# Norms of the keys taken per pair of heads, group norm's Newton steps on GpSimd, and a token shift that reads the neighbouring chunk's bank

## The chip, the cores and the metric

The kernel runs on one core of a Trainium2 chip. A core has TensorE (PE, matrix products; PEld is its weight load, which overlaps), VectorE (DVE), ScalarE (ACT) and GpSimd (POOL). SyncE (SP) only issues transfers here, in the order of its queue. The metric is the device time of one execution in microseconds; the time before is a median of three, 1370.82 us (1363.31 to 1373.83).

## The reference

One layer of a hybrid decoder for a prompt of 1024 tokens and 8 sequences of 4 sample tokens: RWKV-7 time mixing beside dilated sliding-window attention, a gated merge and a closing layer norm, all in fp32. What the change touches:

```python
h = x @ w_in                                            # 1024 -> 9344 columns
prev = concat([shift_prev[:, None], zs[:, :-1]], axis=1)
zs_mixed = zs + mu_shift * (prev - zs)                  # token shift of r, k, v, decay, a
# rwkv_mix, 8 heads of 64 columns
kk = (k * k_k).reshape(B, T, 8, 64)
kk = kk / maximum(norm(kk, axis=-1, keepdims=True), 1e-12)   # keys' norm
k = k * (1.0 + (a - 1.0) * k_a)
S = (S * w_t + (S @ -kk_t) (kk_t * a_t) + v_t k_t)      # one state per head, token by token
o_t = S @ r_t
mu, var = mean(o), mean(square(o - mu))                 # over the 64 columns of a head
o = (o - mu) * rsqrt(var + GN_EPS) * lnx_g + lnx_b      # group norm
y = (o + bonus) * silu(z_gate)
```

## The kernel before

Columns lie on the 128 partitions and tokens along the free side; a tile of 128 columns holds two heads, a pair j of four. The 1056 tokens of prompt and samples are cut into three chunks of 352. The layer has three parts one after the other: the recurrent part (to about 620 us), attention (to about 1184) and the output. The change touches only the first.

A **product** is a group of matmuls at L173 of a 128-column block of the weights with the tokens. Numbers are split into a high and a low part, so three products make one exact one. Weights come by SP (L160) into two buffers `wraw`, are split by ScalarE (`whi`, L163) and VectorE (`wlo`, L164), and 24 matmuls per chunk add up in one of four PSUM banks `pj`. When a chunk is complete, its `consume` takes it out of the bank: `shifted` (L237 to L248) mixes each token with the one before, where the last column of a chunk is kept in a tile `lst` for the next (L239, L241); `silu` (L200) and `gate` (L306) send theirs to DRAM.

Beside the products run four streams, for 8 **units** (pair j, half hf of 512 tokens):

- `units`: `unit` makes the keys' norm (squares, small matmuls against `bones` at L321, `rsqrt` by a seed L151 and three Newton steps L153 to L155 on VectorE, a copy L328 that spreads each norm over its 64 columns, and four PE transposes L344 that turn this into the layout of the keys), the decay and `a` (the lora matmuls L301), then the operands BK (L346 to L355) and KR (L365, L366) and the products AT (L380 on PE, masked by L387 on VectorE; two banks `g` hold them, in two groups of 16 matmuls).
- `inverses`: a triangular inverse in 31 steps on VectorE (L452, L455), which goes through DRAM (Yd, Xd) into AT.
- `scans`: a transposed copy T of the inverse's part (L474), products with it on PE (L487 to L523), and then the scan: 8 chunks of 64 tokens, each with two **hops**. PE multiplies the state `st` with KR (L538), VectorE adds (W, L539), PE multiplies W with BT (L544), VectorE makes the new state in two operations (L547). PE and VectorE wait for each other here, and products are put between.
- `norms`: the group norm of a unit's output on VectorE (L569 to L580), with four PE transposes (L584) behind it.

The order of PE's work is fixed at build time by a planner. Each stream yields a pair: the time that it put on PE, and the time until its next piece is due; products fill what is left. The second number is where the constants stand (`D_KR`, `D_GN` and the like):

```python
streams, prods = [[0.0, scans()], [0.0, norms()], [0.0, inverses()], [0.0, units()]], products()
...
if x[0] <= now and (small < SMALL or x in own or not prods):
    r = next(x[1], 0)
    ...
    now += r[0]
    x[0] = now + r[1]
```

The other engines' order comes from a scheduler that follows what it takes to be ready; each engine, and SP's queue, runs its own strictly in that order. A tile of a pool with few buffers (`t` has six, `nt`, `so` and `srow` one) is waited for until its last reader is done.

Of the kernel before, what the change touches and what calls it, by code (L numbers as in the profile page):

```python
# [14 lines left out]
AF = mybir.ActivationFunctionType  # L15
ALU = mybir.AluOpType
AX = mybir.AxisListType

P = 128
D = 1024  # L20
KT = D // P
SEQ = 1024
# [10 lines left out]
D_PM, D_HOP, D_ST, D_GN, D_IN, D_U0, D_MASK = 0.9, 1.25, 1.75, 12.6, 11.0, 1.2, 1.2  # L33
# [51 lines left out]
def tile_layer(ctx: ExitStack, tc: tile.TileContext, A: dict, O: list):  # L85
# [64 lines left out]
    def rsqrt(y, x, t):  # L150
        V.tensor_scalar(y.bitcast(I32), x.bitcast(I32), -0.5, float(0x5F3759DF), ALU.mult, ALU.add)  # L151
        for _ in range(3):
            V.scalar_tensor_tensor(t, y, -0.5, x, ALU.mult, ALU.mult)  # L153
            V.tensor_tensor(t, t, y, ALU.mult)
            V.scalar_tensor_tensor(y, t, 1.5, y, ALU.add, ALU.mult)  # L155
# [74 lines left out]
    def shifted(s, M):  # L230
        mu, om = prm[:, MU + s : MU + s + 1], der[:, OMM + s : OMM + s + 1]
        lst = mk(rp, [P, 2], "lst", 2)

        def consume(c, b):
            n, t0 = npr(c), c * CH
            S.activation(M[:, t0 : t0 + n], b[:, 0:n], AF.Copy, scale=om)
            V.scalar_tensor_tensor(M[:, t0 + 1 : t0 + n], b[:, 0 : n - 1], mu, M[:, t0 + 1 : t0 + n], ALU.mult, ALU.add)  # L237
            if c:
                V.scalar_tensor_tensor(M[:, t0 : t0 + 1], lst[:, c - 1 : c], mu, M[:, t0 : t0 + 1], ALU.mult, ALU.add)  # L239
            if c < 2:  # L240
                V.tensor_copy(lst[:, c : c + 1], b[:, n - 1 : n])  # L241
            else:
# [69 lines left out]
    def unit(j, hf, M, st, out):  # L312
# [4 lines left out]
        sq = t_()  # L317
        S.activation(sq[:], Mk[:, sl], AF.Square, scale=prm[:, KK + j : KK + j + 1])
        pn = ps("g")
        for c2 in range(4):  # L320
            T.matmul(pn[:, 2 * c2 : 2 * c2 + 2], sq[:, c2 * P : (c2 + 1) * P], bones[:, 0:P:64], start=True, stop=True)  # L321
        yield (0.4, 0.6)
        nt = mk(rp, [P, 24], "nt", 1)
        n2, rn, tn = nt[:, 0:8], nt[:, 8:16], nt[:, 16:24]
        V.tensor_scalar(n2, pn[:, 0:8], 1e-24, None, ALU.max)
        rsqrt(rn, n2, tn)
        rb = t_()
        V.tensor_copy(rb.rearrange("p (a b) -> p a b", a=8), rn.unsqueeze(2).to_broadcast([P, 8, 64]))  # L328
        pw, pa = ps("g"), ps("g")
        lora(((pw[:], 0, j), (pa[:], 1, j)), sl)  # L330
        yield (1.3, D_PN)
        sg = t_()
# [8 lines left out]
        yield (0.0, D_KR)  # L341
        pn = ps("g")
        for c2 in range(4):
            T.transpose(pn[:, c2 * P : (c2 + 1) * P], rb[:, c2 * P : (c2 + 1) * P], ident)  # L344
        kkn = t_()
        V.scalar_tensor_tensor(kkn[:], Mk[:, sl], prm[:, KK + j : KK + j + 1], pn[:], ALU.mult, ALU.mult)  # L346
# [9 lines left out]
        yield (0.45, 0.0)  # L356
# [207 lines left out]
    def norm(j, hf, Ot, bon):  # L564
# [5 lines left out]
        V.tensor_scalar(m8[:], m8[:], 1.0 / 64.0, None, ALU.mult)  # L570
# [901 lines left out]
```

## Time and profile before

| | before |
|---|---|
| three runs | 1363.31, 1370.82, 1373.83 us |
| profiled execution | 1366.1 us |
| its span, first to last instruction | 1364.2 us |
| mean granted clock of PE | 0.994 |
| PE, VectorE, ScalarE, GpSimd busy | 97%, 59%, 34%, 5% |

The span is 1.9 us shorter than the profiled execution, and that execution lies 4.7 us below the median of the three. Rows of a timeline give start, duration, engine, line, operation, tiles written and read, shapes and a count; what stands in brackets is the idle time before it and what ended that. A wait is put down to what came last. Busy times of PE overlap slightly from row to row.

### The profile page before, as it was taken

Reading aid. Unit: us, or ns where it says so; the run is one execution under the profiler, and the core shown is the slowest. Engines: PE = TensorE matmul, PEld = TensorE weight load, DVE = VectorE, ACT = ScalarE, POOL = GpSimd, SP = SyncE. Lnnn points to the kernel's source line nnn. Section 1 sums busy time; section 2 is a strip of 40 time slices with the busy share of each in tenths; the row PEclk is TensorE's granted clock in tenths of the full one; section 3 lists DMA queues with packets and bytes.
Section 4 is the critical chain, followed back from the end, with each engine's and each line's share of the span. In section 5 each row is a group of like instructions: output and inputs, shape, how many; then the busy total and the mean of one; then the engine's idle time right before and its main releaser. Section 6 shows DMA issues by size and latency. Waiting matters only on the chain.

```text
span 1364.2 us, 25930 instructions
## 1 busy us (share of the span) xinstructions
PE 1328.3 (97%) x10097; PEld 1240.9 (91%) x10097; DVE 805.4 (59%) x2203; ACT 469.4 (34%) x1065; POOL 65.5 (5%) x82
## 2 busy tenths in 40 slices
PE   8999999999999999999999999999999999999997
PEld 7998999898988999999999999999999998899786
DVE  5677668786576855543554385437543844665565
ACT  5334344434443443422332323232332234132211
POOL 0000000000000000000000000000000000024100
PEclk9999999999999999999999999999999999999999
DMA  6122223122322233328545465545555656795221
GB/s 208 46 61 66 67 86 97 52 74 69 97 61 80 73 109 95 93 93 156 105 109 120 118 133 102 123 128 129 100 120 129 129 124 156 235 287 165 83 100 68
DMA packets 340151, 151.64 MB, mean 111 GB/s; under 512 B 188808, under 2 KB 329502, under 8 KB 339774
## 3 DMA queue, kind: packets, MB, share of 16 engines
q1 hardware_dynamic: 241150, 129.68, 34.9%
q10 hardware_dynamic: 98880, 20.32, 7.5%
q8 instruction: 79, 1.29, 0.4%
q14 instruction: 42, 0.34, 0.1%
HBM read 110.68 MB, written 38.97 MB: 110 GB/s over the span
## 4 chain that ended last, share of the span: by engine, by line
PE 80%; DVE 12%; DMA 4%; issue 1%; SPq 1%; ACT 1%; ACTq 0%; DVEq 0%
PE pj L173 58%; PE pj L1426 7%; PE o L980 2%; PE s L943 2%; DVE tm L452 2%; DVE X L455 2%; PE t L963 1%; PE g L380 1%; PE s L1062 1%; DMA wraw<-in_w_in_dram 1%; DVE wlo L164 1%; DVE st L547 1%; PE sc L538 1%; DMA cb<-cd 1%; PE sc L544 1%
## 5 line engine op out<-in xcount | busy, mean ns | idle before, releaser
L173 PE MATMUL pj<-xhi,whi 128*128 128x352 f32 x1848 | 398.2, 336 | 4.3 <-ACT xhi L1293 3.2
L173 PE MATMUL pj<-xhi,wlo 128*128 128x352 f32 x1848 | 386.2, 330 | 0.0
L173 PE MATMUL pj<-xlo,whi 128*128 128x352 f32 x1848 | 380.3, 327 | 0.0
L173 PEld LDWEIGHTS pj<-xhi,whi 128*128 128x128 f32 x1848 | 304.0, 189 | 20.5 <-issue 10.4
L173 PEld LDWEIGHTS pj<-xhi,wlo 128*128 128x128 f32 x1848 | 307.2, 190 | 3.9 <-issue 2.3
L173 PEld LDWEIGHTS pj<-xlo,whi 128*128 128x128 f32 x1848 | 308.8, 189 | 1.8 <-issue 0.7
L164 DVE TENSOR_TENSOR wlo<-wraw,whi 128x512 fp32r<-128x512 f32 x162 | 112.7, 697 | 89.8 <-ACT whi L163 89.2
L163 ACT ACTIVATE whi<-wraw 128x512 fp32r<-128x512 f32 x162 | 100.5, 625 | 132.8 <-PE pj L173 87.2
L953 ACT ACTIVATE Sm<-Sm,nm 128x128 f32<-128x128 f32 (+1 forms) x96 | 42.4, 442 | 101.9 <-DVE nm L950 101.9
L452 DVE TENSOR_TENSOR tm<-Y,X 128x60 f32<-128x60 f32 (+24 forms) x248 | 52.2, 210 | 11.1 <-DMA Y<-Yd 4.7
L455 DVE TENSOR_TENSOR X<-X,tm 128x60 f32<-128x60 f32 (+24 forms) x248 | 52.0, 210 | 6.0
L547 DVE SCALAR_TENSOR_TENSOR st<-sc,E,SD 64x64 f32<-64x64 f32 x128 | 36.1, 282 | 29.5 <-PE sc L544 27.8
L945 DVE CUSTOM_DVE_ANT_0 Sm<-s,cst 128x128 f32<-128x128 f32 (+1 forms) x96 | 29.2, 347 | 40.5 <-PE s L943 39.9
L1426 PE MATMUL pj<-wl,mh 128*128 128x512 f32 (+1 forms) x136 | 52.0, 382 | 0.0
L536 ACT ACTIVATE SD<-st,E 128x128 f32<-128x128 f32 x64 | 25.6, 400 | 71.0 <-DVE st L547 70.8
L806 POOL TENSOR_TENSOR kvp<-vv,kv 128x512 f32<-128x512 f32 x16 | 19.7, 1234 | 471.1 <-DVE Ss L814 387.8
L980 PE MATMUL o<-PT,Vt 128*128 128x128 f32 x280 | 38.8, 276 | 0.8 <-ACT PT L967 0.8
L868 ACT ACTIVATE k<-pj 128x352 f32<-128x352 f32 (+1 forms) x36 | 16.2, 454 | 66.1 <-PE pj L173 66.1
L943 PE MATMUL s<-k,q 128*128 128x128 f32 (+1 forms) x192 | 37.7, 325 | 0.7 <-DVE ml L945 0.7
L980 PEld LDWEIGHTS o<-PT,Vt 128*128 128x128 f32 x280 | 36.4, 191 | 1.5 <-ACT PT L967 1.1
L306 ACT ACTIVATE zt<-pj,der 128x352 f32<-128x352 f32 x48 | 26.5, 552 | 31.8 <-PE pj L173 26.5
L540 ACT ACTIVATE Ot<-sc 64x128 f32<-64x128 f32 x64 | 17.3, 270 | 53.3 <-DVE W L539 53.0
(320 smaller groups left out, 1697.6 us busy)
## 6 DMA issues: line engine op xcount, KB each, us to landing
wraw<-in_w_in_dram SPq DMA_DIRECT2D x146, 256.0 KB
gd<-zt SPq DMA_DIRECT2D x48, 176.0 KB
gt<-gd SPq DMA_DIRECT2D x48, 176.0 KB
vs<-bt ACTq DMA_DIRECT2D x48, 128.0 KB
kc<-in_cache_kv_g_dram SPq DMA_DIRECT2D x48, 128.0 KB
Vt<-vs ACTq DMA_DIRECT2D x12, 512.0 KB
cb<-cd SPq DMA_DIRECT2D x12, 512.0 KB
zd<-zt SPq DMA_DIRECT2D x24, 176.0 KB
```

The lines of the kernel that those rows point to most:

```text
L163: S.activation(hi[:], raw[:], AF.Copy)
L164: V.tensor_tensor(lo[:], raw[:], hi.bitcast(F32)[:], ALU.subtract)
L173: T.matmul(out, w[wi][:, n % 4, :], x[:, n % 4, :], start=first and n == 0, stop=last and n == 11)
L306: S.activation(t[:], b[:], AF.Tanh, scale=0.5, bias=der[:, HB + col : HB + col + 1])
L452: V.tensor_tensor(tm, Y[:, r : r + 1, r + 1 : 32].to_broadcast([P, m, n]), X[:, 0:m, r : r + 1].to_broadcast([P, m, n]), ALU.mult)
L455: V.tensor_tensor(X[:, 0:m, r + 1 : 32], X[:, 0:m, r + 1 : 32], tm, ALU.subtract)
L547: V.scalar_tensor_tensor(S1[d, d], pS[d, d], E[d, c, 64:65], SD[d, d], ALU.mult, ALU.add)
L943: T.matmul(r, qT[:, i * P : (i + 1) * P], kT[:, keys[i][0] * P : keys[i][0] * P + n], start=True, stop=True)
L945: V.tensor_tensor_reduce(out=Sm[:, i, 0:n], in0=r, in1=m3 if g == 2 else m12[:, 256 - n : 256], scale=1.0, scalar=NEG, op0=ALU.add, op1=AL ...
L953: S.activation(Sm[:, i, 0:n], Sm[:, i, 0:n], AF.Exp, scale=SCALE, bias=nm[:, x : x + 1], accum_out=ml[:, g, 1, i : i + 1])
L980: T.matmul(po[:, (i % 4) * P : (i % 4 + 1) * P], st["Vt"][:, kb_, :], PT[:, n * P : (n + 1) * P], start=m == 0, stop=m == len(keys[i]) - 1,)
L1426: T.matmul(pb[:], a[:, k], wk, start=x == 0, stop=x == len(prods) - 1)
```

## The change

Three things are changed.

*Keys' norm.* The squares' sums of both halves of a pair are taken together when the first half is due, 16 rows of 128 tokens in all; the tile is transposed by one matmul to [16 x 128], its reciprocal root is taken in that layout, and the result is written to DRAM (`nd`). Each half then reads it back by two transfers that broadcast one head's row over 64 partitions (`rb`). The copy and the four transposes are gone. The planner gets a new constant D_ROW for the time that the way takes.

*Group norm.* The division by 64 and the subtraction are one operation. The three Newton steps, four operations each, are on GpSimd; the seed and the multiply stay on VectorE, and the stream yields between them.

*Token shift.* The first column of a chunk reads the last column of the neighbouring chunk straight from that chunk's PSUM bank; the copies into `lst` are gone.

```diff
--- before.py
+++ after.py
@@ -30,7 +30,7 @@
 
 PIECE = 3
 D_PN, D_KR, D_AT, D_G, D_W, D_INV, D_UP = 0.65, 1.81, 4.5, 0.2, 2.09, 1.3, 8.4
-D_PM, D_HOP, D_ST, D_GN, D_IN, D_U0, D_MASK = 0.9, 1.25, 1.75, 12.6, 11.0, 1.2, 1.2
+D_PM, D_HOP, D_ST, D_GN, D_IN, D_U0, D_MASK, D_ROW = 0.9, 1.25, 1.75, 12.6, 11.0, 1.2, 1.2, 5.0
 SMALL = 1.0
 RS = 8
 CDEC = math.exp(-0.5)
@@ -147,9 +147,15 @@
             V.tensor_tensor(xlo[h][:, :, sl], bv, hi.bitcast(F32), ALU.subtract)
 
 
-    def rsqrt(y, x, t):
+    def rsqrt(y, x, t, pool=False):
         V.tensor_scalar(y.bitcast(I32), x.bitcast(I32), -0.5, float(0x5F3759DF), ALU.mult, ALU.add)
         for _ in range(3):
+            if pool:
+                G.tensor_tensor(t, y, y, ALU.mult)
+                G.tensor_tensor(t, t, x, ALU.mult)
+                G.tensor_scalar(t, t, -0.5, 1.5, ALU.mult, ALU.add)
+                G.tensor_tensor(y, y, t, ALU.mult)
+                continue
             V.scalar_tensor_tensor(t, y, -0.5, x, ALU.mult, ALU.mult)
             V.tensor_tensor(t, t, y, ALU.mult)
             V.scalar_tensor_tensor(y, t, 1.5, y, ALU.add, ALU.mult)
@@ -229,17 +235,16 @@
 
     def shifted(s, M):
         mu, om = prm[:, MU + s : MU + s + 1], der[:, OMM + s : OMM + s + 1]
-        lst = mk(rp, [P, 2], "lst", 2)
+        banks = {}
 
         def consume(c, b):
             n, t0 = npr(c), c * CH
+            banks[c] = b
             S.activation(M[:, t0 : t0 + n], b[:, 0:n], AF.Copy, scale=om)
             V.scalar_tensor_tensor(M[:, t0 + 1 : t0 + n], b[:, 0 : n - 1], mu, M[:, t0 + 1 : t0 + n], ALU.mult, ALU.add)
             if c:
-                V.scalar_tensor_tensor(M[:, t0 : t0 + 1], lst[:, c - 1 : c], mu, M[:, t0 : t0 + 1], ALU.mult, ALU.add)
-            if c < 2:
-                V.tensor_copy(lst[:, c : c + 1], b[:, n - 1 : n])
-            else:
+                V.scalar_tensor_tensor(M[:, t0 : t0 + 1], banks[c - 1][:, CH - 1 : CH], mu, M[:, t0 : t0 + 1], ALU.mult, ALU.add)
+            if c == 2:
                 bs = b[:, n:CH].rearrange("p (b t) -> p b t", t=NT)
                 ms = sM[:, s, :].rearrange("p (b t) -> p b t", t=NT)
                 S.activation(sM[:, s, :], b[:, n:CH], AF.Copy, scale=om)
@@ -314,21 +319,31 @@
         sl = slice(512 * hf, 512 * hf + 512)
         t_ = lambda tag="t", n=6: mk(rp, [P, 512], tag, n)
         c2p = lambda a: a.rearrange("p (a b c) -> p a b c", a=4, b=2)
-        sq = t_()
-        S.activation(sq[:], Mk[:, sl], AF.Square, scale=prm[:, KK + j : KK + j + 1])
-        pn = ps("g")
-        for c2 in range(4):
-            T.matmul(pn[:, 2 * c2 : 2 * c2 + 2], sq[:, c2 * P : (c2 + 1) * P], bones[:, 0:P:64], start=True, stop=True)
-        yield (0.4, 0.6)
-        nt = mk(rp, [P, 24], "nt", 1)
-        n2, rn, tn = nt[:, 0:8], nt[:, 8:16], nt[:, 16:24]
-        V.tensor_scalar(n2, pn[:, 0:8], 1e-24, None, ALU.max)
-        rsqrt(rn, n2, tn)
-        rb = t_()
-        V.tensor_copy(rb.rearrange("p (a b) -> p a b", a=8), rn.unsqueeze(2).to_broadcast([P, 8, 64]))
+
+        if hf == 0:
+            pn = ps("g")
+            for x in range(2):
+                sq = t_()
+                S.activation(sq[:], Mk[:, 512 * x : 512 * x + 512], AF.Square, scale=prm[:, KK + j : KK + j + 1])
+                for c2 in range(4):
+                    n = 4 * x + c2
+                    T.matmul(pn[:, n:16:8], sq[:, c2 * P : (c2 + 1) * P], bones[:, 0:P:64], start=True, stop=True)
+                yield (0.8, 0.4)
+            n2 = mk(rp, [P, 16], "n2", 1)
+            V.tensor_scalar(n2[:], pn[:, 0:16], 1e-24, None, ALU.max)
+            yield (0.0, 0.6)
+            pn = ps("g")
+            T.transpose(pn[0:16, 0:P], n2[:], ident)
+            yield (0.1, 0.4)
+            rn, tn = mk(rp, [P, P], "so", 1), mk(rp, [P, P], "srow", 1)
+            rsqrt(rn[0:16, :], pn[0:16, 0:P], tn[0:16, :])
+            SP.dma_start(nd[j].rearrange("e (c p) -> (e c) p", p=P), rn[0:16, :])
         pw, pa = ps("g"), ps("g")
         lora(((pw[:], 0, j), (pa[:], 1, j)), sl)
         yield (1.3, D_PN)
+        rb = t_()
+        for e in range(2):
+            SP.dma_start(rb[64 * e : 64 * e + 64, :], nd[j, e : e + 1, sl].to_broadcast([64, 512]))
         sg = t_()
         S.activation(sg[:], pw[:], AF.Tanh, scale=0.5, bias=der[:, HW0 + j : HW0 + j + 1])
         ta = t_()
@@ -338,12 +353,9 @@
         V.tensor_tensor_scan(lam[:], rmask, sg[:], 0.0, ALU.mult, ALU.add)
         Ei = t_()
         S.activation(Ei[:], lam[:], AF.Exp, scale=0.5 * CDEC)
-        yield (0.0, D_KR)
-        pn = ps("g")
-        for c2 in range(4):
-            T.transpose(pn[:, c2 * P : (c2 + 1) * P], rb[:, c2 * P : (c2 + 1) * P], ident)
+        yield (0.0, D_KR + D_ROW / 3 if hf else D_KR + D_ROW)
         kkn = t_()
-        V.scalar_tensor_tensor(kkn[:], Mk[:, sl], prm[:, KK + j : KK + j + 1], pn[:], ALU.mult, ALU.mult)
+        V.scalar_tensor_tensor(kkn[:], Mk[:, sl], prm[:, KK + j : KK + j + 1], rb[:], ALU.mult, ALU.mult)
         bt = t_()
         V.scalar_tensor_tensor(bt[:], ta[:], 1.0, kkn[:], ALU.add, ALU.mult)
         f2 = t_()
@@ -353,7 +365,6 @@
         BK = mk(rp, [P, 4, 4, 64], "BK", 1)
         V.scalar_tensor_tensor(BK[:, :, 1:3, :], c2p(bt), 0.5, c2p(Ei), ALU.mult, ALU.mult)
         V.tensor_tensor(BK[:, :, 0:4:3, :], c2p(k2), c2p(Ei), ALU.mult)
-        yield (0.45, 0.0)
         while done["scan"] < 2 * j + hf - 1 or 0 not in M:
             yield None
         Mr = M[0]
@@ -567,8 +578,7 @@
         Og = Ot.rearrange("p a (b c) -> p (a b) c", b=2)
         m8 = mk(rp, [P, 8], "m8", 1)
         V.tensor_reduce(m8[:], Og, AX.X, ALU.add)
-        V.tensor_scalar(m8[:], m8[:], 1.0 / 64.0, None, ALU.mult)
-        V.tensor_tensor(Og, Og, m8.unsqueeze(2).to_broadcast([P, 8, 64]), ALU.subtract)
+        V.scalar_tensor_tensor(Og, m8.unsqueeze(2).to_broadcast([P, 8, 64]), -1.0 / 64.0, Og, ALU.mult, ALU.add)
         sq = t_("sz", 2)
         S.activation(sq[:], Ot.rearrange("p a b -> p (a b)"), AF.Square)
         v8 = mk(rp, [P, 8], "v8", 1)
@@ -576,9 +586,10 @@
         V.tensor_scalar(v8[:], v8[:], 1.0 / 64.0, GN_EPS, ALU.mult, ALU.add)
         nt = mk(rp, [P, 24], "nt", 1)
         r8 = nt[:, 0:8]
-        rsqrt(r8, v8[:], nt[:, 8:16])
+        rsqrt(r8, v8[:], nt[:, 8:16], True)
+        yield (0.0, 3.0)
         V.tensor_tensor(Og, Og, r8.unsqueeze(2).to_broadcast([P, 8, 64]), ALU.mult)
-        yield (0.0, D_GN)
+        yield (0.0, D_GN - 3.0)
         po = ps("g")
         for c2 in range(4):
             T.transpose(po[:, c2 * P : (c2 + 1) * P], Ot[:, c2, :], ident)
@@ -606,6 +617,7 @@
     pbc = lambda o: prm[:, o : o + 4].unsqueeze(2).to_broadcast([P, 4, NS])
     dbc = lambda o: der[:, o : o + 4].unsqueeze(2).to_broadcast([P, 4, NS])
     bns = mk(cpool, [P, 4, NS], "bns")
+    nd = mk(dpool, [4, 2, SEQ], "nd")
     vd = mk(dpool, [8, NS, 6, 64], "vd")
```

The order on the engines, before and then after, at three places. First VectorE at the first unit's group norm. `Ot` is the unit's output, `v` the variance, `nt` the tile of the root, `AT` the masked products of a later unit, `zt` a gate and `wlo` a weight split. Before, with the last of the three Newton steps at its head:

```order
L153 SCALAR_TENSOR_TENSOR nt_2080<-nt_2080,v_371_2077 128x8
L154 TENSOR_TENSOR nt_2080<-nt_2080 128x8
L155 SCALAR_TENSOR_TENSOR nt_2080<-nt_2080 128x8
L580 TENSOR_TENSOR Ot_1568<-Ot_1568,nt_2080 128x512
L200 SCALAR_TENSOR_TENSOR zt_2134<-zt_2135,pj_2017 128x352
L387 TENSOR_TENSOR AT_2143<-g_2144,cst_76 128x512
L387 TENSOR_TENSOR AT_2143<-g_2145,cst_76 128x512
L200 SCALAR_TENSOR_TENSOR zt_2164<-zt_2165,pj_2018 128x352
```

and after:

```order
L586 TENSOR_SCALAR v_366_2056<-v_366_2056 128x8
L151 TENSOR_SCALAR nt_2059<-v_366_2056 128x8
L206 SCALAR_TENSOR_TENSOR zt_2103<-zt_2104,pj_1975 128x352
L591 TENSOR_TENSOR Ot_1561<-Ot_1561,nt_2059 128x512
L206 SCALAR_TENSOR_TENSOR zt_2121<-zt_2122,pj_1976 128x352
L398 TENSOR_TENSOR AT_2130<-g_2131,cst_76 128x512
L398 TENSOR_TENSOR AT_2130<-g_2132,cst_76 128x512
L206 SCALAR_TENSOR_TENSOR zt_2151<-zt_2152,pj_1977 128x352
L170 TENSOR_TENSOR wlo_2449<-wraw_2446,whi_2448 128x512
```

No Newton step stands on VectorE between the seed (L151) and the multiply (L591) any longer, but one gate; the masks (L398) still follow the multiply.

Second VectorE at the keys of the third pair's second half, in the scan beside them, from one W on. `tm` and `X` belong to an inverse, `m` to the token shift, `BK` and the `t` tiles to the keys. Before:

```order
L539 TENSOR_TENSOR W_3162<-sc_4180,R_585_3257 64x128
L452 TENSOR_TENSOR tm_4325<-Y_4069,X_4074 128x70
L164 TENSOR_TENSOR wlo_4361<-wraw_4358,whi_4360 128x512
L346 SCALAR_TENSOR_TENSOR t_4195<-m_1680,prm_90,g_4190 128x512
L455 TENSOR_TENSOR X_4074<-X_4074,tm_4325 128x5x14
L348 SCALAR_TENSOR_TENSOR t_4197<-t_4147,t_4195 128x512
L547 SCALAR_TENSOR_TENSOR st_124_780<-sc_4214,E_2913,SD_4178 64x64
L352 TENSOR_TENSOR t_4201<-m_1680,t_4199 128x512
L354 SCALAR_TENSOR_TENSOR BK_4203<-t_4197,t_4152 128x4x128
L355 TENSOR_TENSOR BK_4203<-t_4201,t_4152 128x4x2x64
L547 SCALAR_TENSOR_TENSOR st_124_780<-sc_4214,E_2913,SD_4178 64x64
```

and after, from the keys' multiply (L358) on, with the next state one row further:

```order
L358 SCALAR_TENSOR_TENSOR t_4193<-m_1641,prm_90,t_4135 128x512
L466 TENSOR_TENSOR X_3997<-X_3997,tm_4212 128x5x15
L360 SCALAR_TENSOR_TENSOR t_4195<-t_4140,t_4193 128x512
L558 SCALAR_TENSOR_TENSOR st_123_775<-sc_4151,E_2869,SD_4106 64x64 x2
L364 TENSOR_TENSOR t_4199<-m_1641,t_4197 128x512
L366 SCALAR_TENSOR_TENSOR BK_4201<-t_4195,t_4145 128x4x128
L550 TENSOR_TENSOR W_3141<-sc_4175,R_586_3251 64x128
L367 TENSOR_TENSOR BK_4201<-t_4199,t_4145 128x4x2x64
L463 TENSOR_TENSOR tm_4215<-Y_3992,X_3997 128x70
L170 TENSOR_TENSOR wlo_4309<-wraw_4306,whi_4308 128x512
L466 TENSOR_TENSOR X_3997<-X_3997,tm_4215 128x5x14
L379 SCALAR_TENSOR_TENSOR t_4468<-m_2884,prm_90,t_4199 128x512
```

The block (L346 to L355 before, L358 to L367 after) lay between one W and the second operation of its state; now the state (L558) of the W ahead of it and the next W (L550) stand inside it. The norm of the same pair stands some 130 rows ahead, in an earlier scan, behind this W:

```order
L550 TENSOR_TENSOR W_2340<-sc_3358,R_442_2468 64x128
L151 TENSOR_SCALAR so_3381<-g_3368 16x128
L463 TENSOR_TENSOR tm_3409<-Y_3188,X_3193 128x70
L159 SCALAR_TENSOR_TENSOR srow_3382<-so_3381,g_3368 16x128
L466 TENSOR_TENSOR X_3193<-X_3193,tm_3409 128x5x14
L160 TENSOR_TENSOR srow_3382<-srow_3382,so_3381 16x128
L244 SCALAR_TENSOR_TENSOR m_3123<-pj_3126,prm_90,m_3123 128x319
L246 SCALAR_TENSOR_TENSOR m_3123<-pj_3125,prm_90,m_3123 128x1
L161 SCALAR_TENSOR_TENSOR so_3381<-srow_3382,so_3381 16x128
L463 TENSOR_TENSOR tm_3456<-Y_3188,X_3193 128x65
```

The seed and the Newton steps on [16 x 128] tiles (`so`, `srow`) alternate with an inverse and with rows of the shift, and the next state comes 26 rows behind the W.

Third SP's queue around the same pair, after (before, there was no transfer for the norm):

```order
L166 DMA wraw_3608<-in_w_in_dram 128x4x128
L166 DMA wraw_3705<-in_w_in_dram 128x4x128
L340 DMA nd_373<-so_3381 16x128
L166 DMA wraw_3819<-in_w_in_dram 128x4x128
L346 DMA t_3430<-nd_373 64x512 x2
L166 DMA wraw_3959<-in_w_in_dram 128x4x128
L346 DMA t_4135<-nd_373 64x512
L470 DMA Xd_570_3183<-X_3193 256x1x32 x4
L346 DMA t_4135<-nd_373 64x512
L166 DMA wraw_4115<-in_w_in_dram 128x4x128
L484 DMA AT_2923<-Xd_570_3183 32x8x32 x4
```

The write of `nd` and the four reads into `t` tiles stand among the weight loads (L166), and two of the reads next to the transfer of the inverse (L470).

## The prediction

> **What bounds the kernel now.** I read the page first, then busy time by stretches, then what TensorE (PE) waits for, then single rows.
>
> ```profile
> span 1364.2 us, 25930 instructions
> PE 1328.3 (97%) x10097; PEld 1240.9 (91%) x10097; DVE 805.4 (59%) x2203; ACT 469.4 (34%) x1065; POOL 65.5 (5%) x82
> PE 80%; DVE 12%; DMA 4%; issue 1%; SPq 1%; ACT 1%; ACTq 0%; DVEq 0%
> ```
>
> PE is busy for 97% of the span, and holds 80% of the chain that ends last; all other engines have room on average. So an edit pays if it takes work off PE, or takes away a wait in which PE stands still. The change touches only the recurrent phase, which ends before 620 us. Busy time in stretches of it (stretch, length, busy PE, PEld, DVE, ACT, POOL, then the granted clock of PE, the DMA share and GB/s):
>
> ```profile
> 120.00:140.00 20.00, 18.82 (x214) 17.76 (x215) 17.30 (x71) 8.31 (x19) 0.00 (x0) 0.91 0.10 28
> 320.00:340.00 20.00, 17.26 (x102) 16.10 (x101) 17.49 (x67) 8.13 (x17) 0.00 (x0) 0.91 0.13 43
> 20.00:620.00 600.00, 585.95 (x5090) 552.75 (x5090) 399.37 (x1332) 247.73 (x529) 5.92 (x20) 0.99 0.28 79
> ```
>
> PE is idle for 600 - 585.95 = 14.05 us in these 600. Twice the granted clock falls to 0.91, which costs 0.09 x 20 = 1.8 us each time, 3.6 in all. What PE waits for in the same 600 us (us in total, times, longest):
>
> ```profile
> PE sc L538 <- DVE st L547: 7.0, 8, 2.3
> PE sc L487 <- DVE T L474: 3.3, 3, 2.1
> PE sc L544 <- DVE W L539: 2.3, 3, 1.1
> PE g L380 <- DVE AT L387: 0.6, 2, 0.4
> PE g L380 <- DVE BK L355: 0.6, 1, 0.6
> ```
>
> Together 13.8 us, nearly all of the idle time, and all of it for VectorE (DVE). 9.3 belong to the scan's hops (L538 and L544 on PE, W at L539 and st at L547 on DVE), 3.3 to the start of a scan, where PE wants the transposed inverse T. The largest single ones:
>
> ```profile
> 121.18 0.71 PE L487 MATMUL sc<-T,AT 32*32 32x32 f32 x30 [2.15 <-DVE T L474]
> 332.87 0.46 PE L538 MATMUL sc<-st,KR 128*128 128x128 f32 x2 [2.27 <-DVE st L547]
> 333.08 1.30 PE L173 MATMUL pj<-xhi,whi 128*128 128x352 f32 x4
> ```
>
> These two stand in the two stretches with the low clock. Behind the second, four products take 1.30 us where they take 0.65 elsewhere (row below). The Trainium skill's "TensorE: Matmul & The Clock Gate", Part 1, "What's actually happening", has the gate fall to half rate after an idle window of about 3.4 us that runs freely. Here it fell after 2.15 and 2.27 us; I go by the rows and take idle times of about 2 us as able to cost 1.8 us more.
>
> So the change can win at most the 13.8 us of waits, the 3.6 of clock, and what it takes off PE. About 1% of the time, 13.7 us, is what a measurement of this kernel tells from no change.
>
> **Keys' norm: work off PE.** From the chain that ended last (start, length, what):
>
> ```profile
> 100.22 0.65 PE pj L173 x4
> 112.10 0.91 PE g L301 x6
> 117.05 0.45 PE g L344 x4
> ```
>
> The four transposes of the spread norms (L344), 0.45 us for each of 8 units, go: 3.6 us. For each of 4 pairs one transpose of [128x16] comes, at 0.45 / 4 = 0.11: 0.45 us. The 64 small norm matmuls stay. PE has no cover, so this is **-3.1 us**. On DVE the copy L328 and nine of twenty operations on norms go; nothing waits for them there.
>
> **Scan start: T.** T waits for the inverse, 62 operations on DVE. In the changed order fewer DVE rows stand between them (half as many Newton steps, no copies of the shift), and PE's regular order puts the T products about as far behind the end of each inverse as they need. I take 0.5 us of the 3.3 as left (the first pair, where SP issues the nd write and the two broadcasts near the loads of AT): **-2.8 us**; all 3.3 may stay.
>
> **Hops.** DVE from W to the second st of the hop with the 2.27 us wait:
>
> ```profile
> 327.73 0.30 DVE L539 TENSOR_TENSOR W<-sc,R 64x128 f32<-64x128 f32 x1
> 328.06 0.23 DVE L452 TENSOR_TENSOR tm<-Y,X 128x70 f32<-128x70 f32 x1
> 328.21 0.69 DVE L164 TENSOR_TENSOR wlo<-wraw,whi 128x512 fp32r<-128x512 f32 x1
> 328.92 0.75 DVE L346 SCALAR_TENSOR_TENSOR t<-m,prm,g 128x512 f32<-128x512 f32 x1
> ...
> 330.33 0.27 DVE L547 SCALAR_TENSOR_TENSOR st<-sc,E,SD 64x64 f32<-64x64 f32 x1
> ...
> 332.43 0.29 DVE L547 SCALAR_TENSOR_TENSOR st<-sc,E,SD 64x64 f32<-64x64 f32 x1
> ```
>
> From 327.73 to 332.72 DVE needs 5.0 us, because a weight split and the block L346 to L355 lie inside the hop. In the changed order that block is spread over two hops, so this wait should go. But for the pairs whose norm now falls inside a scan, one hop holds the ten operations of the new rsqrt on [16x128] tiles. The nearest rows are those of the same code on 128 elements a row:
>
> ```profile
> 553.30 0.29 DVE L155 SCALAR_TENSOR_TENSOR t<-t 128x128 f32<-128x128 f32 x1
> 553.51 0.68 DVE L164 TENSOR_TENSOR wlo<-wraw,whi 128x512 fp32r<-128x512 f32 x1
> ```
>
> Such an operation lets the next, independent one start 0.21 later; one of the inverse (328.06) does so after 0.15. Ten of each, in turns, take 2.1 + 1.5 us; the split of 0.69 and five small rows of the shift, put at 0.3 each, make it 5.8 us. PE has 0.11 + 0.65 + 0.91 + 3 x 0.65 = 3.6 us to do meanwhile (the transpose, four products, six lora matmuls, twelve products). So it waits 2.2 us, once in each of two pairs: 4.4. The other hops lose the block, and I leave them 2 of their 7: 6.4 of the 9.3 stay, **-2.9 us**, between -9.3 and, if the new waits pull the clock down as the old ones did (1.8 each), +0.7.
>
> **Group norm's Newton steps.** Seed to multiply in the first unit on DVE, and the PE row that the masks behind it hold up:
>
> ```profile
> 172.12 0.17 DVE L151 TENSOR_SCALAR nt<-v 128x8 int32<-128x8 int32 x1
> 172.32 0.17 DVE L153 SCALAR_TENSOR_TENSOR nt<-nt,v 128x8 f32<-128x8 f32 x1
> ...
> 174.62 0.69 DVE L580 TENSOR_TENSOR Ot<-Ot,nt 128x512 f32<-128x512 f32 x1
> ...
> 175.75 1.29 DVE L387 TENSOR_TENSOR AT<-g,cst 128x512 f32<-128x512 f32 x2
> 177.79 0.94 PE L380 MATMUL g<-KR,BK 64*128 64x128 f32 x12
> ```
>
> Nine operations take from 172.32 to 174.62, 2.3 us, with one weight split among them. Now twelve on GpSimd take their place, and the multiply stands right behind the seed in DVE's order, with none to two other rows between. DVE is in order, so it stands still until GpSimd is done; behind it wait the masks (L387), which free the two banks that PE's second group of AT products (177.79) writes. The masks end at 177.04: 0.75 us of slack here, and none in the two places where the list of waits has L380 behind AT L387. GpSimd never worked on 8 elements a row but to fill them:
>
> ```profile
> 417.19 0.11 POOL L361 MEMSET E<- 128x8 f32 x1 [3.54 <-DVE st L547]
> ...
> 549.87 0.41 POOL L639 TENSOR_TENSOR m<-m,der 128x128 f32<-128x128 f32 x1
> 550.37 0.47 POOL L640 TENSOR_TENSOR m<-m,sM 128x128 f32<-128x128 f32 x1
> 682.08 1.04 POOL L806 TENSOR_TENSOR kvp<-vv,kv 128x512 f32<-128x512 f32 x1 [16.27 <-DVE Ss L814]
> ```
>
> 0.41 at 128 elements and 1.04 at 512 lie on a line that has 0.22 at 8; dependent operations start 0.50 apart where one takes 0.41, 0.09 more. That is 0.30 for a step, between 0.20 (the fill and the gap) and 0.50 (the spacing as it stands). Twelve at 0.30 are 3.6 us, 1.3 later than now; the dropped operation L570 gives back 0.2, and a row that stood behind the multiply and is now inside gives 0.5 to 0.7 where there is one. Against the slack I take 0.4 us of wait in each of the six units that have masks behind them: **+2.4 us**. At 0.20 a step it is 0. At 0.50, 6.0 us, each unit waits about 2.8: +17.
>
> [...]
>
> **The way through DRAM.** One write of [16x128] and two broadcasts for each half, on SP's queue. The nearest ways through DRAM (start, length), and the waits of the weight loads in SP's queue:
>
> ```profile
> 481.91 3.74 DMA AT<-Xd
> 1049.21 6.27 DMA cb<-cd
> 1161.27 1.85 DMA t<-ml
> 1165.21 4.56 DMA cd<-nE
> SPq L160 <- DVE wlo L164: 134.1, 30, 18.3
> ```
>
> Write and read take between 1.85 + 3.74 = 5.6 and 4.56 + 6.27 = 10.8 us. I take 5.6, since the tile is only 8 KB. In the pairs inside a scan DVE has sixteen operations of the inverse at 0.15, a split at 0.69, four st and a W at 0.3 and two rows of full width at 0.7 between the last rsqrt operation and the first reader of rb, 6.0 us: it waits for nothing. At 10.8 it stands still for 5 us there, with a hop's W and st behind it. The weight loads on SP behind the nd write wait 134.1 / 30 = 4.5 us on average for their own buffers now, which covers a few us of waiting ahead of them. Taken as **0**, at most +15 for three pairs.
>
> **Token shift.** The copy of the last column goes:
>
> ```profile
> L241 DVE COPY lst<-pj 128x1 f32<-128x1 f32 x26 | 3.9, 150 | 0.0
> ```
>
> 3.9 us of DVE that no PE wait was put down to: 0. In return a bank of PSUM is held until the next chunk's shift has run, some 2 us longer (twelve products are 1.94); PE has four banks and comes back to this one a chunk later. It shows only where DVE lags by more than about 1.7 us: 0, at worst a microsecond in each of the few hops where DVE is that late.
>
> **Sum.** -3.1 - 2.8 - 2.9 + 2.4 = -6.4, so the profiled execution, 1366.1 with 1.9 around its span, becomes 1359.7. It stood 4.7 below the median of 1370.8; by the median the forecast is 1364.
>
> **The rivals.** *The waits all go.* With fewer DVE rows and hops in step, none of the 13.8 us and neither fall of the clock returns: -3.1 - 13.8 - 3.6 = -20.5, 1350; half of the relief gives 1357. For it: DVE is 67% busy in this phase and loses some 15 us of rows. Against it: the ten new operations inside one hop.
>
> *GpSimd's chain becomes the bound.* At 0.50 a step the sum is -8.8 + 17 = +8, and with idle times of 2.8 us the clock falls too: 1.8 in each of up to six units, +19 in all, 1390. It decides from about 0.27 a step, where the slack is used up; from 0.36 it eats the whole gain, and past 0.42 the kernel is over 1% slower. For it: the row spacing at 128 elements; against it: the 0.11 us fill of 8.
>
> *The broadcast comes late.* +15 for three pairs against -6.4: about +9, 1380. *Nothing moves:* the waits only change places, and PE's 3.1 us is within what cannot be told, 1368.
>
> **How the numbers follow.** Forecast (1357 to 1372, with the last rival inside it, which differs by less than the range) 0.59; all waits go 0.22; GpSimd bound 0.12; late broadcast 0.07. Faster by over 1% (below 1357) takes the first rival and a little of the forecast's edge, 0.24; slower by over 1% (above 1384.5) takes most of the second rival and part of the third, 0.13; the rest, 0.63, is no change. The range leaves out the best tenth of the first rival's gains and the worst of the second: 1352 to 1378.
>
> **What will show it.** Right: no L344 row; L487 behind T under 1 us in all; GpSimd's twelve operations at 0.30 each, and 0.2 to 0.6 us of wait before the second AT products; one wait of about 2 us on st in the hop that holds the new rsqrt. Wrong: GpSimd steps of 0.4 and more with DVE idle behind the seed, DVE rows that wait for the DMA from nd, PE waiting for a bank pj, or a granted clock below 0.95 in more than two stretches.

## The result, and the profile after

The changed kernel takes 1376.79 us (median of eight runs, 1374.98 to 1379.02), the kernel before 1368.37 beside it (1363.31 to 1373.83). The ratio is 1.007, 95% interval 1.0057 to 1.0084: slower by 0.7%, 8.4 us, where 1364 was forecast. It lies inside the range and within 1%, on the other side. The profiled execution took 1377.07 us.

The page of the changed kernel: span and busy times.

```profile
span 1375.3 us, 25865 instructions
PE 1336.3 (97%) x10069; PEld 1244.7 (91%) x10069; DVE 787.9 (57%) x2045; ACT 471.3 (34%) x1065; POOL 88.1 (6%) x178
```

There are 28 matmuls fewer on PE, 32 transposes less four, and VectorE works 17.5 us less, but PE is busy for 8.0 us more. What PE waits for from 20 to 640 us (us in total, times, longest):

```profile
PE g L306 <- DVE srow L159: 9.3, 4, 3.3
PE sc L549 <- DVE st L558: 5.0, 9, 1.2
PE g L391 <- DVE AT L398: 1.4, 3, 0.7
PE sc L508 <- ACT T L504: 0.5, 2, 0.3
PE g L306 <- DVE Ot L570: 0.3, 1, 0.3
PE sc L555 <- DVE W L550: 0.3, 1, 0.3
```

The old waits are shorter: hops from 9.3 to 5.3 us, T from 3.3 to none. Part of that is only that PE now stands still elsewhere; with the new wait removed (the copy, below) hops and T come back to 7.9. A new one of 9.3 us, four times, stands at the head: the lora matmuls (L306, L301 before) wait for the Newton steps of the keys' norm (L159). The third of the four on PE (start, length, idle time in brackets), then VectorE at the same time:

```profile
273.78 0.49 PE L306 MATMUL g<-lorh,lhi 64*128 64x512 f32 x1
277.58 0.79 PE L306 MATMUL g<-lorh,lhi 64*128 64x512 f32 x1 [3.31 <-DVE srow L159]
...
279.60 1.52 PE L179 MATMUL pj<-xhi,whi 128*128 128x352 f32 x4
...
284.18 0.81 PE L179 MATMUL pj<-xhi,wlo 128*128 128x352 f32 x4
```

```profile
273.97 0.28 DVE L151 TENSOR_SCALAR so<-g 16x128 int32<-16x128 int32 x1
...
274.43 0.27 DVE L159 SCALAR_TENSOR_TENSOR srow<-so,g 16x128 f32<-16x128 f32 x1
...
277.26 0.27 DVE L159 SCALAR_TENSOR_TENSOR srow<-so,g 16x128 f32<-16x128 f32 x1
```

The second operand of L159 is `g`: the root reads the transposed norms where PE left them, in one of the two PSUM banks `g`, in each of its three steps. The lora matmuls need both banks. The first goes (273.78), the second waits until the third L159 (277.26 to 277.53) has read, and starts at 277.58. Behind it a row of four products takes 1.52 us, where such a row takes 0.81 from 284.18 on. The granted clock in the stretches where it fell (its column is the third from the right):

```profile
120.00:140.00 20.00, 19.54 (x219) 17.58 (x218) 15.11 (x49) 10.34 (x21) 0.00 (x0) 0.93 0.28 82
260.00:280.00 20.00, 16.69 (x131) 15.19 (x130) 16.86 (x76) 6.22 (x15) 0.00 (x0) 0.91 0.08 22
280.00:300.00 20.00, 19.28 (x138) 18.73 (x138) 17.31 (x51) 8.18 (x18) 0.11 (x1) 0.92 0.30 75
400.00:420.00 20.00, 18.06 (x113) 17.43 (x114) 17.26 (x63) 8.89 (x19) 0.41 (x2) 0.91 0.20 57
540.00:560.00 20.00, 19.60 (x180) 18.44 (x179) 10.59 (x28) 8.19 (x22) 5.03 (x18) 0.91 0.24 72
```

The shortfalls, 0.07 + 0.09 + 0.08 + 0.09 + 0.09, make 8.4 us of lost clock, where the kernel before lost 3.6. The first four, 6.6 us together, stand at or right behind waits on L306, which end at 119, 278 and 402 us. The fifth stands behind no such wait (last section).

GpSimd in the first group norm, and VectorE's wait for it over the eight norms:

```profile
177.89 0.20 POOL L154 TENSOR_TENSOR nt<-nt 128x8 f32<-128x8 f32 x1 [6.81 <-DVE nt L151]
178.17 0.21 POOL L155 TENSOR_TENSOR nt<-nt,v 128x8 f32<-128x8 f32 x1
...
181.00 0.20 POOL L157 TENSOR_TENSOR nt<-nt 128x8 f32<-128x8 f32 x1
```

```profile
DVE Ot L591 <- POOL nt L157: 23.4, 8, 4.3
```

Twelve steps from 177.89 to 181.20 are 3.31 us, 0.28 a step. VectorE stands still in front of the multiply for 23.4 us in all.

The way through DRAM, in SP's queue at the third pair:

```profile
278.24 0.33 SPq L340 DMA_DIRECT2D nd<-so  x1
...
279.59 1.12 SPq L346 DMA_DIRECT2D t<-nd  x2
```

The reads, which need the write, are issued 1.35 us after it; at the other pairs it is 1.38, 1.40 and 2.55. No row of VectorE's list of waits names a transfer from `nd`.

### The profile page after: what moved, and what is told of

The parts are those of the page before. It is cut to its first block, busy times and chain, and to the rows that moved or that the text cites. A ratio compares the mean times of both kernels' runs of the same rounds, so it can differ in the third digit from the quotient of the medians.

```text
span 1375.3 us, 25865 instructions
## 1 busy us (share of the span) xinstructions
PE 1336.3 (97%) x10069; PEld 1244.7 (91%) x10069; DVE 787.9 (57%) x2045; ACT 471.3 (34%) x1065; POOL 88.1 (6%) x178
## 4 chain that ended last, share of the span: by engine, by line
PE 76%; DVE 13%; DMA 4%; issue 3%; ACT 1%; POOL 1%; SPq 1%; DVEq 0%; ACTq 0%; POOLq 0%
PE pj L179 54%; PE pj L1438 7%; PE o L992 2%; PE s L955 2%; DVE tm L463 2%; DVE X L466 2%; DMA cb<-cd 2%; DVE wlo L170 1%; PE t L975 1%; PE s L1074 1%; DVE st L558 1%; PE sc L549 1%; PE g L391 1%; PE sc L555 1%; DVE o L1238 1%
## 5 line engine op out<-in xcount | busy, mean ns | idle before, releaser
L179 PE MATMUL pj<-xhi,whi 128*128 128x352 f32 x1848 | 403.7, 340 | 3.7 <-ACT xhi L1305 3.2
L558 DVE SCALAR_TENSOR_TENSOR st<-sc,E,SD 64x64 f32<-64x64 f32 x128 | 36.1, 282 | 26.5 <-PE sc L555 25.0
```

The lines of the kernel that those rows point to most:

```text
L179: T.matmul(out, w[wi][:, n % 4, :], x[:, n % 4, :], start=first and n == 0, stop=last and n == 11)
L558: V.scalar_tensor_tensor(S1[d, d], pS[d, d], E[d, c, 64:65], SD[d, d], ALU.mult, ALU.add)
```

## The experiments

Each kernel was timed beside the kernel before, which had medians of 1365.9 to 1367.1 us here, against 1368.4 beside the changed kernel. Ratios are to the kernel before that was timed beside the same kernel.

**The bank released by a copy.** After the transpose, one VectorE operation more:

```diff
-            rsqrt(rn[0:16, :], pn[0:16, 0:P], tn[0:16, :])
+            xs = mk(rp, [P, P], "xs", 1)
+            V.tensor_copy(xs[0:16, :], pn[0:16, 0:P])
+            rsqrt(rn[0:16, :], xs[0:16, :], tn[0:16, :])
```

> The changed kernel with one edit: the transposed norms are copied from their PSUM bank g to SBUF by one VectorE operation, and the reciprocal root reads the copy, so the bank comes free after the copy and not after the last Newton step. PE's order is the same. Theory of the bank: PE's second lora matmul waits 9.3 us in all for that bank and the low clock behind it costs about 8 more; the wait on L306 falls under 1.5 us, the waits for st grow by at most 3, the granted clock comes back to 0.994 or more, and the time is about 1361 (0.995 of the kernel before). Rival, the chain: the ten operations of the root hold up VectorE itself, so that the wait only moves to st behind them, some 2 us per pair with the same low clock behind, and the time stays at 1373 to 1377.

1367.61 us, 1.0005 of the kernel before (0.9994 to 1.0017), 9.2 less than the changed kernel. PE's waits:

```profile
PE sc L551 <- DVE st L560: 5.6, 10, 1.2
PE g L393 <- DVE AT L400: 3.3, 5, 2.0
PE sc L557 <- DVE W L552: 1.6, 3, 1.1
PE g L668 <- POOL m L649: 1.2, 1, 1.2
PE sc L500 <- DVE T L487: 0.7, 1, 0.7
PE g L668 <- DVE m L651: 0.3, 1, 0.3
```

The wait on L306 is gone, and that on st did not take its place (5.0 to 5.6 us): the bank, not the root's chain in front of the next state, carried the loss. The time did not reach 1361, so something else costs too; the list names the masks (L400), whose wait grew from 1.4 to 3.3.

The 9.2 us are not 9.2 us of wait. All waits listed fall only from 16.8 to 12.7, since PE now meets others sooner: W (0.3 to 1.6), the masks, T (0.7) and the sample rows L668 (1.5). The lost clock falls from 8.4 to 1.8 us, one stretch at 0.91. By the two profiles, 10.3 us apart, the clock thus is the larger part.

**PE kept busy while it waits.** Matmuls whose result is overwritten, ahead of the lora matmuls:

```diff
         pw, pa = ps("g"), ps("g")
+        if hf == 0:
+            for _ in range(16):
+                T.matmul(pw[:], lhi[0:64, P * j : P * j + P], lorh[0:64, sl], start=True, stop=True)
         lora(((pw[:], 0, j), (pa[:], 1, j)), sl)
```

> The changed kernel with 16 matmuls more (some 2.4 us) ahead of the lora matmuls of each pair's first half, into the bank that is free already; their result is overwritten. The bank g is held as long as in the changed kernel, but PE is not idle while it waits for it. Theory that idle time of 2 to 3 us pulls the clock down and that this costs as much as the wait: the wait on L306 falls from 9.3 to about 1.5 us, the clock comes back to 0.994, no stretch but one or two under 0.95, and the time falls by 6 to 9 us against the changed kernel, to about 1369, although no useful work is done sooner. Rival, the low clock has another cause: the time stays at 1376 or rises by 1 to 2 us.

1375.41 us, 1.0068 (1.0056 to 1.008): only 1.4 less, and so a miss by its time. The 16 matmuls of a pair took longer than the 2.4 us that I had put down (14.4 us for the four pairs, where the wait was 9.3), so their number was then fitted to each pair's wait:

```diff
-            for _ in range(16):
+            for _ in range((6, 7, 14, 11)[j]):
```

> The changed kernel with 6, 7, 14 and 11 overwritten matmuls ahead of the lora matmuls of the four pairs, cut to the length of the wait for the bank g (0.22 to 0.24 us each, where the first such kernel had 16 for each pair and 14.4 us in all against 9.3 of wait). PE then is busy in place of idle for nearly the same time. Theory that the idle time pulls the clock down: no stretch under 0.95, the time falls by 5 to 7 us against the changed kernel, to 1370 to 1372. Rival, the low clock is not the idle time's doing or costs little: 1375 to 1377.

1371.95 us, 1.0035 (1.0023 to 1.0048), 4.8 less than the changed kernel although more is computed and the bank is held as long. The wait on L306 and the first of the same stretches:

```profile
PE g L306 <- DVE srow L159: 0.3, 2, 0.2
```

```profile
120.00:140.00 20.00, 19.50 (x226) 17.80 (x225) 16.57 (x55) 10.45 (x22) 0.00 (x0) 1.00 0.27 82
```

The clock stays at 1.00 in this one and in the next three. The overwritten matmuls take 9.1 us and leave 0.3 of wait, so PE starts its useful work no sooner. The idle time thus cost about half as much again by the clock as by itself: 4.8 us by the medians, 6.2 between the two profiled spans, beside 9.3.

**Products while the bank is held.** A yield lets the planner put products between the root and the lora matmuls:

```diff
             SP.dma_start(nd[j].rearrange("e (c p) -> (e c) p", p=P), rn[0:16, :])
+            yield (0.0, 5.0)
         pw, pa = ps("g"), ps("g")
```

> The changed kernel with a yield of 5 us of the planner between the root and the lora matmuls, so that PE does products while the bank g is held by the root. The bank is held as long as before. Theory of the bank: the wait on L306 falls under 1.5 us, and the time comes to 1361 to 1366, if the decay and BK behind the later lora matmuls are still in time. Rival, the chain: waits of about 2 us per pair show on st in its place, 1372 to 1377.

1368.84 us, 1.0014 (1.0002 to 1.0026), with no wait on L306, 7.9 us on st and 4.4 on the masks. Like the copy it takes back most of the 8.4 us, by filling the wait and not by shortening it. The time lies between the theory's and the rival's, so this run alone would not decide between them.

**Both other parts without the keys' norm.** The kernel before with the group norm's and the shift's part:

> The kernel before with the other two parts of the change alone (Newton steps of the group norm on GpSimd with its two yields, the shift that reads the neighbouring bank); the keys' norm is as before. If the keys' norm carries the loss: no wait on a bank g for the lora matmuls, 1 to 2 us of wait for the masks, and a time of 1366 to 1371, as the kernel before. Rival, GpSimd's chain or the held PSUM banks pj carry it: 1374 or more, with the waits on L391 or on pj.

1373.3 us, 1.0054 (1.0036 to 1.0072): a miss. The other parts lose 6 us by themselves. Apart:

> The kernel before with the group norm's part of the change alone (merged division and subtraction, Newton steps on GpSimd, the two yields). GpSimd's step takes 0.285 us in the changed kernel, twelve 3.4, and PE's second AT products then wait 1.4 to 3.3 us in all. Theory that these waits are the part's whole price: 1 to 2 us slower than before, 1368 to 1369. Rival, the part carries the 6 us that both parts without the keys' norm lost: 1372 to 1374, with more low clock behind the masks' waits.

> The kernel before with the shift that reads the neighbouring bank, and the merged division of the group norm; keys' norm and Newton steps as before. PE's order is that of the kernel before, only VectorE's and the release of the banks pj differ. Theory that the held bank costs nothing: within 2 us of the kernel before, 1365 to 1368. Rival, it carries the 6 us that both parts without the keys' norm lost: 1372 to 1374, with waits on pj or longer waits on st and T.

With the group norm's part alone 1374.59 us, 1.0063 (1.0043 to 1.0084); with the shift 1366.49, 0.9998 (0.9985 to 1.0012). So the held banks pj cost nothing, and the Newton steps on GpSimd with their yields cost 7.7 us, 0.6 more than the rival of the expectation. The wait for the masks grows from 0.6 to 2.5 there and that for T from 3.3 to 4.7. Then, beside the copy, the Newton steps back on VectorE, and the keys' part alone:

```diff
-        rsqrt(r8, v8[:], nt[:, 8:16], True)
-        yield (0.0, 3.0)
+        rsqrt(r8, v8[:], nt[:, 8:16])
...
-        yield (0.0, D_GN - 3.0)
+        yield (0.0, D_GN)
```

> The changed kernel with the bank g released by a copy, and the group norm's Newton steps back on VectorE without the added yield. If GpSimd's chain costs what the masks' waits show, 2 to 3 us less than with the copy alone: 1364 to 1366. If it costs the 6 us of both parts: 1361 to 1362. Rival, the wait only moves, since VectorE gets its rows back: 1367 to 1369.

> The kernel before with the keys' part of the change alone (with the merged division of the group norm), and the bank g released by a copy; the shift and the Newton steps are as before. By the terms of the prediction, -3.1 for PE's transposes, -2.8 for T and -2.9 for the hops, it takes 1358 to 1360, if the copies of the shift cost nothing. Rival, the terms for T and the hops were the shift's and the Newton steps' gain, rows that VectorE loses: only PE's 3.1 us are left, 1363 to 1365.

1357.98 us, 0.9934 (0.9918 to 0.995), for the copy without GpSimd's steps, 9.6 less than with them; and 1360.32, 0.9953 (0.9937 to 0.9969), for the keys' part alone. The first lies below every value expected for it, the second 0.3 above its range. The first is faster than both kernels, and the two together say that the shift's dropped copies are worth some 2 us beside the keys' part, where alone they showed nothing. Waits of the first:

```profile
PE sc L551 <- DVE st L560: 5.7, 10, 1.1
PE sc L557 <- DVE W L552: 1.6, 3, 1.1
PE sc L500 <- DVE T L487: 1.3, 2, 0.7
PE g L393 <- DVE AT L400: 0.6, 2, 0.3
```

Against the list of the copy alone, 2.7 us of the masks' wait and the 1.5 of the sample rows (L668) are gone. More of it hides inside a row. PE's group of AT products from the timeline and all of them by line, with the Newton steps on VectorE and then, for the copy alone, on GpSimd:

```profile
296.81 1.75 PE L393 MATMUL g<-KR,BK 64*128 64x128 f32 x16 [0.32 <-DVE AT L400]
L393 PE MATMUL g<-KR,BK 64*128 64x128 f32 x256 | 19.6, 285 | 0.8 <-DVE AT L400 0.6
```

```profile
299.65 1.75 PE L393 MATMUL g<-KR,BK 64*128 64x128 f32 x16 [1.97 <-DVE AT L400]
300.25 0.96 PEld L393 LDWEIGHTS g<-KR,BK 64*128 64x128 f32 x14 [0.30 <-DVE AT L400]
L393 PE MATMUL g<-KR,BK 64*128 64x128 f32 x256 | 21.9, 287 | 4.0 <-DVE AT L400 3.3
```

A group that had to wait lasts 1.75 us in place of 1.16: after two of the 16 matmuls the weight loads wait for the second mask (300.25). Five groups are that long with GpSimd (1.67 to 1.75) and one without. That is another 2.3 us. VectorE at the norm of the third unit, Newton steps on VectorE and then on GpSimd:

```profile
293.45 0.17 DVE L151 TENSOR_SCALAR nt<-v 128x8 int32<-128x8 int32 x1
...
295.46 0.69 DVE L592 TENSOR_TENSOR Ot<-Ot,nt 128x512 f32<-128x512 f32 x1
296.07 1.28 DVE L400 TENSOR_TENSOR AT<-g,cst 128x512 f32<-128x512 f32 x2
```

```profile
294.66 0.17 DVE L151 TENSOR_SCALAR nt<-v 128x8 int32<-128x8 int32 x1
298.30 0.69 DVE L593 TENSOR_TENSOR Ot<-Ot,nt 128x512 f32<-128x512 f32 x1 [3.48 <-POOL nt L157]
298.91 1.28 DVE L400 TENSOR_TENSOR AT<-g,cst 128x512 f32<-128x512 f32 x2
```

From seed to multiply it is 2.01 us on VectorE and 3.64 with GpSimd, and the masks come 1.63 later. Two causes were left: the masks queued behind the multiply, and the planner's other order with the added yield.

> The changed kernel with the bank g released by a copy, and the group norm's multiply behind the Newton steps moved from VectorE to GpSimd. The twelve steps on GpSimd stay as long (3.4 us), but VectorE no longer has an operation in its queue that waits for them, so the masks go ahead. Theory that the group norm's part costs 9.6 us because the masks queue behind the multiply: the waits on L393 fall from 3.3 us to under 0.5, and the time comes from 1367.6 to 1357 to 1359, as with the Newton steps on VectorE. Rival, GpSimd's work itself slows VectorE or holds up the sample rows: 1364 or more.

> The changed kernel with the bank g released by a copy, and the Newton steps back on VectorE, but with the yield of 3 us between them and the multiply kept, so that PE's order is that of the changed kernel. If GpSimd's chain carries the 9.6 us: 1357 to 1359, as without the yield. Rival, the yield's other order on PE carries it: 1365 or more.

The multiply on GpSimd as well (one letter, `V` to `G`, in the line of the multiply), so that VectorE has nothing in its queue that waits: 1360.8 us, 0.9955 (0.994 to 0.997). The yield kept and the Newton steps on VectorE: 1359.5 us, 0.9944 (0.9928 to 0.9959). Of the 9.6 us, 6.8 come back when VectorE no longer waits, although GpSimd does even more, and 8.1 when the chain goes and the order stays. So the masks behind the multiply carry most of it, and the yield's order 1.5; what is left of GpSimd's own part stays open. The first ran 1.8 us above its expectation, the second 0.5. Waits with the multiply on GpSimd:

```profile
PE sc L500 <- DVE T L487: 2.3, 3, 1.4
...
PE g L393 <- DVE AT L400: 0.2, 1, 0.2
```

**The fourth corner.** The changed kernel with the Newton steps on VectorE, without the copy:

> The changed kernel with the group norm's Newton steps back on VectorE, without the added yield, and the bank g held by the root as in the change: the fourth corner beside the changed kernel (1376.8), the copy (1367.6) and the copy without GpSimd's steps (1358.0). If the two losses add up, the bank's 9 us and GpSimd's 9 us stand apart: 1366 to 1368, the time of the kernel before, with 9 us of wait on L306 again. Rival, the two feed each other (a late VectorE lengthens the root and so the wait for the bank): 1361 to 1364.

1369.05 us, 1.0015 (1.0001 to 1.0029), with 9.3 us of wait on L306 again. The four corners, in us:

| | Newton steps on GpSimd | on VectorE |
|---|---|---|
| bank g held by the root | 1376.8 | 1369.1 |
| bank g released by a copy | 1367.6 | 1358.0 |

The bank costs 9.2 and 11.1, GpSimd 7.7 and 9.6. By the ratios it is 8.9 and 11.1, 7.5 and 9.7. They add up to within 2 us, which is about what the intervals leave open; the fourth corner came 1 us above its expectation.

## Why the prediction was wrong

**The step that failed first** stands under "Hops": "PE has 0.11 + 0.65 + 0.91 + 3 x 0.65 = 3.6 us to do meanwhile (the transpose, four products, six lora matmuls, twelve products)". The 0.91 of the lora matmuls, and all that is behind them in PE's order, could not run meanwhile. They write both banks `g`, and one of them is read by the very rsqrt that they were to cover. I had counted the operations of the root and not asked which buffer they read, and had looked for a PSUM cost of the change under the token shift (banks `pj`) and behind the masks, not here. In place of 2.2 us in front of st in each of two pairs, PE waited 1.5 to 3.3 us in front of the lora matmuls in each of four.

With the copy the lora matmuls run, and the waits for st and W are 7.2 us in all, near the 6.4 put down, but not where they were put. The root of the third pair stands at 269.79 to 274.50 us on VectorE there, with two states and a W inside, and the only wait of PE from 269 to 283 is

```profile
279.80 0.49 PE L557 MATMUL sc<-W,BT 128*128 128x128 f32 x2 [0.26 <-DVE W L552]
```

The other hops kept about 7 us in place of 2, so it is luck that the totals agree. Whether the 2.2 us would have come with VectorE's order as it stood is not shown, since the copy changes that order too. In the changed kernel the next state comes so far behind its W because PE's product with that W (L555, at 279.15) stands behind the lora matmuls of 277.58; the working took it for the length of the root alone.

**The price of GpSimd's chain** was the second, a size: +2.4 was put down and 7.7 to 9.6 measured. The step was right, 0.30 against 0.28. The wait per unit was not. I took the first unit's 2.3 us from the first Newton step to the multiply for all. From the seed that is 2.5, where the third unit, above, has 2.0 without GpSimd and 3.6 with it, and the slack of 0.75 us before the second AT products, read in the first unit, is absent there. So the term that was put down at 2.4, the masks, measures 5.0 in the two profiles beside the copy: 2.7 us of wait for them and 2.3 inside the groups of AT products. What had been put at nothing comes on top: 1.5 for the sample rows (that the last norms hold these up in the same queues is not shown), and one fall of the clock:

```profile
300.00:320.00 20.00, 19.89 (x233) 17.83 (x232) 7.89 (x20) 9.59 (x20) 0.00 (x0) 0.91 0.34 92
```

That is 1.8 more, 8.3 together; the wait for T is 0.6 shorter, which leaves 7.7 of the 9.0 between the two spans, 1365.0 and 1356.0. The rival "GpSimd's chain becomes the bound" named this mechanism and its threshold of 0.27 a step, but took the gain to be eaten from 0.36 on; it was eaten at 0.28. Its 0.36 does not come out of its own figures either: from 2.4 at 0.30 to 17 at 0.50 the cost reaches 8.8 at 0.39. The low end of the step, 0.20, is the busy time of a step alone; from one dependent step to the next it is 0.28.

**The clock was counted as unchanged** and lost 8.4 us in place of 3.6. The working had 1.8 us for each idle time of about 2 us in hand and used it only in a bound of the hops and in the rivals. Behind the waits on L306 stood 6.6 us of it. The prediction's own sign of being wrong, a clock below 0.95 in more than two stretches, came up.

**What held, and what only agrees.** PE's transposes, T and the hops together were -8.8; the changed kernel with the copy and the Newton steps on VectorE measures -8.9 against the kernel before. The terms do not bear this out one by one. T kept 1.3 us and not 0.5, the hops 7.3 and not 6.4; against that the waits in front of the AT products went from 1.2 to 0.6, and both falls of the clock went, 3.6 that was counted at nothing. With 3.1 for the transposes, which no run shows apart, this would be -11.3, so 2.4 us are open and the agreement is luck. The way through DRAM is hidden, as forecast. Its lower bound of 1.85 for the write was read from a transfer between two tiles that both lie on the chip (`t<-ml`); a write to `nd` and the dependent read are 1.35 to 2.55 apart. The shift costs nothing.

Smaller slips changed no term: the 0.65 of four undisturbed products is a piece of the chain, and the timeline row to set beside 1.30 is 0.81; ten, not nine, of a pair's twenty root operations go; half of the relief in the first rival gives 1359, not 1357; and 1% is not what a measurement here needs, since the interval of the ratio is 0.14% to each side.

**The sum with what the runs showed:** -8.9 for the keys and the shift, +9.6 for GpSimd beside the copy, +9.2 for the bank and its clock, together +9.9. These are differences along the four corners, so they must give 1376.8 - 1366.9; the 8.4 measured is against the 1368.4 that the kernel before took beside the changed kernel. That the time lies inside the range comes of two losses of some 9 us each against a gain of 9, and not of the terms.

## What to carry to other kernels

When an operand in PSUM is read by a chain of operations, the bank is held for the whole chain: ask who needs that bank next, and copy a small operand out first (one operation of 0.28 us in each pair took back 9.2 here). Work moved to another engine frees its old engine only if nothing there waits for the result at once; an in-order queue makes everything behind that one operation late (the masks by 1.63 us here). And a wait on a busy PE is to be priced with the clock that may fall behind it.

## What the runs showed of the hardware that was not expected

Idle time on PE of 1.79 to 3.31 us was followed by half speed, at the third pair from 277.58 to about 283 (a row of four products in 1.52 us), and overwritten work in its place kept the clock at 1.00. In all the profiles here, every idle time of 1.79 us or more between 20 and 640 us was followed by such rows. Below that it goes both ways. The wait of 1.48 us at the first pair had no such effect in the changed kernel, and had it in the profile of the fourth corner (whose granted clock reads 0.95 almost throughout, while its rows of four products take the usual 0.81 outside the falls):

```profile
48.08 0.50 PE L306 MATMUL g<-lorh,lhi 64*128 64x512 f32 x1 [1.48 <-DVE srow L159]
```

```profile
47.99 0.50 PE L306 MATMUL g<-lorh,lhi 64*128 64x512 f32 x1 [1.48 <-DVE srow L159]
...
49.81 1.38 PE L179 MATMUL pj<-xhi,wlo 128*128 128x352 f32 x4
```

Two falls came with no idle time above 0.3 us in front of them: the fifth stretch of the changed kernel, from 546.02 on, and the kernel with the multiply on GpSimd from 43.65 on (0.91 from 40 to 60 us):

```profile
543.84 0.28 PE L306 MATMUL g<-lorh,lhi 64*128 64x32 f32 x1 [0.29 <-DVE Ot L570]
...
547.04 1.38 PE L179 MATMUL pj<-xhi,whi 128*128 128x352 f32 x4
```

```profile
42.73 1.05 PE L330 MATMUL g<-cst,t 128*128 128x2 f32 x8
43.65 1.46 PE L179 MATMUL pj<-xlo,whi 128*128 128x352 f32 x4
```

Both stand behind groups of narrow matmuls (32 and 2 columns). Whether these bear on it was not tried; in the other profiles no fall stands behind such groups. And the wait of 2.15 us at the first scan start, which stood at 0.91 in the kernel before, stands at 0.74 in the kernel without the keys' part.

What sets the falls off, and how long they last, stays open. The mean clock of one kernel moves from run to run as well: for the kernel before it was 0.989 to 0.996 over the runs beside the copy. A single profile's clock is therefore not that of the next run, and the comparisons above rest on the timed runs.
